# Group 2's attention keys through the seven-product scheme of the queries and keys stage, with each softmax placed behind the next combination's splits

## The chip, the cores and the metric

One core of a Trainium2 chip runs the whole kernel. The metric is the device time of one execution in microseconds (us); lower is better. TensorE (PE in the profile) multiplies; VectorE (DVE) and ScalarE (ACT) do elementwise work; GpSimd (POOL) does little here and issues some DMAs; SyncE (SP) issues nearly all other DMAs, in order.

## The reference

One decoder block on 1024 tokens of width 1024, in float32: a normed and modulated input `h` is projected by one wide matrix; a retention branch (4 heads) and a dilated sliding-window attention branch run beside each other and are merged by sigmoid gates; a squared-ReLU MLP follows. What matters here is the attention branch and its projections:

```python
ATT_GROUPS = ((128, 1), (512, 4), (2048, 16))     # (window, dilation) of three groups of 4 heads, head width 128
proj = h @ w_in                                    # queries, keys, values of every head, and the gates
for gi, (win, dil) in enumerate(ATT_GROUPS):
    aq, ak, av = parts[4 + 3 * gi], parts[5 + 3 * gi], parts[6 + 3 * gi]
    o, lse = dilated_group(heads(aq, 4), heads(ak, 4), heads(av, 4), tab, win, dil)
wts = softmax(stack(lses), axis=0)                 # the three groups of a head are weighed against each other
att = einsum('gbhs,gbhsd->bshd', wts, o_all)
# inside dilated_group, on the tokens of one residue class modulo the dilation:
s = einsum('bhrnid,bhrnjd->bhrnij', qs, kb) * dh ** -0.5 + bias     # masked to the band
e = exp(s - max(s));  den = sum(e);  lse = max + log(den)
```

## The kernel before, in words

**Precision.** Every large product is computed as three products of split operands: a number is split in a high part (a rounded copy, made on ScalarE) and a low part (the rest, a subtraction on VectorE), and `mm3` (lines 203 to 211) adds weight-low x input-high, weight-high x input-low and weight-high x input-high in PSUM. So each operand that TensorE reads costs one ScalarE and one VectorE operation first: a *split*. A matmul here has 128 x 128 weights and up to 512 columns.

**Stages.** Values first; then `queries_keys` (one long step); then values of the retention; then retention chunk by chunk; then attention; then output projections, merge and MLP.

**The queries and keys stage** computes the retention's queries and keys, all attention queries and a part of the gates in pairs of 256 output columns. A pair is one 2 x 2 block product by a scheme of seven products instead of eight (class `Blocks`, `ORDER`): each product is 4 slices of 3 matmuls, 84 matmuls of 512 columns for a pair; VectorE makes the sums of weight blocks and puts the results together. `PAIRS` is the order of the 18 pairs, written by hand as a string; `a_load` loads the weights of a pair two pairs ahead; `a_out` stores queries of attention to the DRAM tensors `aq_d`, in the order of tokens that their group needs.

**The attention stage** goes twice through the same steps, once for each pair of heads (`pair` 0 and 1; `a` is the head in the pair, `g` the group). A *combination* is (g, a), in the order (1,0), (1,1), (2,0), (2,1), (0,0), (0,1). `att_step` for combination i issues 8 slices of 6 matmuls for its keys (`proj_gen`) and, woven in between from the third slice on (`weave` with `lag=2`), the score matmuls of the combination before (`scores_gen`; bias added by VectorE out of PSUM). Then `k_split` splits the new keys out of PSUM, and `scores_end` does the softmax of the combination before: maximum on VectorE, its negation `ng`, eight exponentials on ScalarE (`P<-P,ng`). Behind the second head of a group, `stats_out` sends the row statistics through DRAM. The first `cover_step` (a projection of gates, n = 0) covers the scores of the last combination; then come the weights of the groups, the scaling of the probabilities, and the products with the values in the further cover steps.

**Order.** Nothing is scheduled by a planner: each engine runs its instructions in the order in which the Python code issues them. Class `Steps` decides when weights and queries are split: `following` runs at the start of a step and issues the splits for the next step, and of the weights that lead the step behind that one. Loads (`raw`, three buffers) are issued when the load three places earlier has been split. SP executes them in order with all other DMAs, so a DMA that waits holds up those behind it.

**Result sums.** 32 DMAs that add up parts of the retention's result (`result_sum`, DRAM to DRAM, issued by POOL) are handed out by `with_sums`: two in each projection of the attention stage.

PSUM in this stage: two double banks for projections (`ps_mm`), four single banks for scores and transposes (`ps_s`). Splits of queries and keys live in a ring of eight buffers (`ring`).

Of the kernel before, what the change touches and what calls it, by code (L numbers as in the profile page):

```python
# [11 lines left out]
F32 = mybir.dt.float32  # L12
# [128 lines left out]
def block_kernel(ctx, tc, io, stop=None, dbg=None):  # L141
# [434 lines left out]
    def with_sums(gen):  # L576

        return at(at(gen, 1, result_sum), 5, result_sum)
# [192 lines left out]
    aq_d = {(p, g, a): dram.tile([P, S], F32, name=f"aqd{p}{g}{a}") for p in range(2) for g in range(3) for a in range(2)}  # L771
    h12_d = [dram.tile([P, 2, 512], F32, name=f"h12d{m}") for m in range(4)]
# [363 lines left out]
    PAIRS = [{"r": r_pairs, "a": a_pairs, "g": g_pairs}[i].pop(0) for i in "rargrargrargrargaa"]  # L1136
# [3 lines left out]
    def a_load(q, part):  # L1140
        pair = PAIRS[q]
        src = io[{"g": "w_gate2", "a": "w_aq"}.get(pair[0]) or f"w_r{pair[1]}"]
# [22 lines left out]
    def a_out(q, n, x, y=None):  # L1165
# [6 lines left out]
        if pair[0] == "a" and pair[1] == 1:  # L1172
            o = OA[q][i].rearrange("p (r n i) -> p r n i", r=4, n=2)[:, :, t, :]
            view = lambda z: z.rearrange("p (i r) -> p r i", r=4)
        elif pair[0] == "a" and pair[1] == 2:
            o = OA[q][i].rearrange("p (r i) -> p r i", r=8)[:, :, 64 * t:64 * t + 64]
            view = lambda z: z.rearrange("p (i r) -> p r i", r=8)
# [7 lines left out]
        if n in ("12", "21"):  # L1185
            if pair[0] == "g":
                dst = gate_d[GATES[2 * pair[1] + i]]
            elif pair[0] == "a":
                dst = aq_d[pair[2], pair[1], i]
            else:  # L1190
# [292 lines left out]

    def k_split(pair, g, a, ps):
# [266 lines left out]
    combos = [(g, a) for g in (1, 2, 0) for a in range(2)]  # L1751

    def att_step(pair, i):

        g, a = combos[i]

        def body(*args):
            ps = ps_mm(f"ak{pair}{i}")
            gen = with_sums(proj_gen(ps, args[-1]))
            if i == len(combos) - 2:  # L1760
                v_fetch(pair, 0)
            if i > 0:
                last = combos[i - 1]
                weave(gen, NK, scores_gen(pair, *last), len(SB[last[0]]), lag=2)
# [11 lines left out]
            else:  # L1776

                gen = at(at(gen, 3, args[0]), NK - 1, lambda: k_split(pair, g, a, ps))
                weave_pv(gen, NK - 1, 0, 2)
            if i == 0:  # L1780
                A["st"] = A["p"].tile([P, 3, 8, 4], F32, tag="st", name=f"st{pair}")
                bias_load(pair)
            if i > 0 or pair == 0:
                k_split(pair, g, a, ps)
            if i > 0:
                scores_end(pair, *last)
                if last[1] == 1:
                    stats_out(pair, last[0])
        return body

    def cover_step(pair, n):
# [4 lines left out]
        def body(*args):  # L1796
            ps = ps_mm(f"gate0{i}")
            gen = with_sums(proj_gen(ps, args[-1]))
            if n == 0:
                v_fetch(pair, 1)  # L1800
                weave(gen, 6, scores_gen(pair, *combos[-1]), len(SB[0]), lag=2, rest=False)
                drain(gen)
                v_split(pair, 0, False)
                scores_end(pair, *combos[-1])
# [38 lines left out]
    for pair in range(2):  # L1843
        for i, (g, a) in enumerate(combos):
            steps.add(att_step(pair, i),
                      [wsplit(io["w_ak"][g * 4 + 2 * pair + a])] +
# [955 lines left out]
```

## Time and profile before

| | us |
|---|---|
| runs shown (3): lowest, median, highest | 2182.08, 2183.38, 2184.13 |
| profiled execution, whole | 2182.64 |
| its span, first to last instruction | 2180.9 |
| TensorE busy in it | 2156.0 |
| VectorE busy | 1491.7 |
| ScalarE busy | 942.8 |

The profiled execution is the one whose rows are quoted; its span is what its rows add up to, and 1.7 us lie around it. Rows of the order in time give start, duration, engine, line of the kernel, operation, output <- inputs, and in brackets the idle time of that engine just before with what ended it. Rows of groups end with busy us, mean ns of one, and the idle time before them.

### The profile page before, as it was taken

How to read it: one execution, taken by the hardware profiler on the slowest of the kernel's cores; microseconds unless marked ns; L12 is line 12 of the kernel's file. 1: busy time of each engine (PE TensorE's matmuls, PEld its weight loads, DVE VectorE, ACT ScalarE, POOL GpSimd, SP SyncE). 2: the span in 40 equal slices, each digit the busy share in tenths (PEclk: the TensorE clock that was granted, in tenths of full speed). 3: DMA queues.
4: the chain of work that ended last, by engine and by line, in shares of the span. 5: the costliest groups of instructions: out<-in, count | busy, mean ns of one | idle time of the engine just before them, and what ended most of it. 6: DMA issues, size and time to landing. Idle time of an engine off the chain costs nothing. (4 is left out here: it accounts for less than half of the span.)

```text
span 2180.9 us, 27323 instructions
## 1 busy us (share of the span) xinstructions
PE 2156.0 (99%) x10084; PEld 1791.6 (82%) x10084; DVE 1491.7 (68%) x2333; ACT 942.8 (43%) x1729; POOL 164.0 (8%) x195
## 2 busy tenths in 40 slices
PE   8999999999999999999999999999999999999998
PEld 6888888888878888888888888888778888888887
DVE  5985777774467877854655644776876665877855
ACT  5553323323434544544644625434454545533413
POOL 0001111100012212211100000001000000000003
PEclk9999999999999999999999999999999999999999
DMA  9859998844685555557763275654254435645322
GB/s 383 289 209 297 296 298 257 243 119 174 237 301 170 198 174 194 181 172 190 184 167 108 81 268 189 224 186 139 65 182 150 153 136 194 249 137 175 111 87 78
DMA packets 160881, 416.78 MB, mean 191 GB/s; under 512 B 27749, under 2 KB 55660, under 8 KB 157676
## 3 DMA queue, kind: packets, MB, share of 16 engines
q1 hardware_dynamic: 151416, 368.67, 47.9%
q0 software_dynamic: 9008, 46.14, 9.9%
q8 instruction: 79, 1.29, 0.2%
q14 instruction: 54, 0.44, 0.1%
q10 hardware_dynamic: 324, 0.23, 0.0%
HBM read 319.93 MB, written 156.13 MB: 218 GB/s over the span
## 5 line engine op out<-in xcount | busy, mean ns | idle before, releaser
L207 PE MATMUL qap<-hh,qaw 128*128 128x512 f32 x216 | 84.0, 389 | 0.0
L209 PE MATMUL qap<-hl,qaw 128*128 128x512 f32 x216 | 84.0, 389 | 0.0
L211 PE MATMUL qap<-hh,qaw 128*128 128x512 f32 x216 | 84.0, 389 | 0.0
L617 POOL TENSOR_TENSOR j<-qk,j 128x512 fp32r<-128x512 f32 x32 | 43.2, 1351 | 412.4 <-ACT j L616 393.8
L2122 POOL TENSOR_TENSOR accnf<-accnf,sqnf 128x256 f32<-128x256 f32 (+1 forms) x18 | 16.6, 922 | 609.9 <-ACT sqnf L2118 609.9
L2226 ACT ACTIVATE a<-a 128x512 f32<-128x512 f32 x48 | 30.3, 631 | 73.7 <-DVE a L2225 73.7
L1542 ACT ACTIVATE P<-P,ng 128x128 f32<-128x128 f32 (+1 forms) x96 | 42.0, 439 | 36.6 <-DVE ng L1539 36.6
L2434 ACT CAST w2h<-w2s 128x512 fp32r<-128x512 f32 x36 | 22.4, 622 | 78.7 <-DVE w2s L2472 78.7
L264 DVE TENSOR_TENSOR fw<-w1r,fw 128x512 fp32r<-128x512 f32 x48 | 32.9, 688 | 33.6 <-ACT fw L254 33.6
L1957 DVE TENSOR_TENSOR rwl<-rwl,rwh 128x1024 fp32r<-128x1024 f32 x25 | 30.2, 1220 | 29.1 <-ACT rwh L1987 29.1
L207 PE MATMUL fp<-h2h,fw 128*128 128x512 f32 x128 | 50.0, 391 | 0.0
L211 PE MATMUL fp<-h2h,fw 128*128 128x512 f32 x128 | 49.8, 389 | 0.0
L209 PE MATMUL fp<-h2l,fw 128*128 128x512 f32 x128 | 49.8, 389 | 0.0
L207 PE MATMUL roa<-rh,rwl 128*128 128x512 f32 x128 | 49.8, 389 | 0.0
L209 PE MATMUL roa<-rl,rwh 128*128 128x512 f32 x128 | 49.8, 389 | 0.0
L211 PE MATMUL roa<-rh,rwh 128*128 128x512 f32 x128 | 49.8, 389 | 0.0
L652 ACT COPY sm<-sT 128x128 f32<-128x128 f32 x32 | 8.5, 266 | 93.7 <-PE sT L640 93.7
L207 PEld LDWEIGHTS qap<-hh,qaw 128*128 128x128 f32 x216 | 40.5, 188 | 8.5
L209 PEld LDWEIGHTS qap<-hl,qaw 128*128 128x128 f32 x216 | 40.5, 188 | 8.4
L211 PEld LDWEIGHTS qap<-hh,qaw 128*128 128x128 f32 x216 | 40.5, 188 | 8.4
L2122 POOL TENSOR_TENSOR accn<-accn,sqn 128x512 f32<-128x512 f32 x12 | 15.5, 1293 | 386.1 <-ACT sqn L2118 386.1
L1947 ACT ACTIVATE rh<-rl 128x512 fp32r<-128x512 f32 x56 | 31.7, 623 | 23.4 <-PE roc L209 8.4
(3097 smaller groups left out, 7251.4 us busy)
## 6 DMA issues: line engine op xcount, KB each, us to landing
v<-vd SPq DMA_DIRECT2D x32, 512.0 KB, 4.5
raw<-in_w_ada_dram SPq DMA_DIRECT2D x32, 512.0 KB, 5.3
w1r<-in_w_ff_dram SPq DMA_DIRECT2D x32, 512.0 KB, 4.6
yt<-y POOLq DMA_DIRECT2D x24, 512.0 KB, 7.6
xsd<-as SPq DMA_DIRECT2D x24, 512.0 KB, 2.8
w2r<-in_w_ff2s_dram SPq DMA_DIRECT2D x24, 512.0 KB, 6.9
em<-in_w_ada_dram SPq DMA_DIRECT2D x16, 512.0 KB, 10.2
wrvs<-in_w_rv_dram POOLq DMA_DIRECT2D x16, 512.0 KB, 10.0
```

The lines of the kernel that those rows point to most:

```text
L207: nc.tensor.matmul(o, wl, xh, start=first, stop=False, skip_group_check=skip)
L209: nc.tensor.matmul(o, wh, xl, start=False, stop=False, skip_group_check=skip)
L211: nc.tensor.matmul(o, wh, xh, start=False, stop=last, skip_group_check=skip)
L264: nc.vector.tensor_sub(t[:, 512:], src, fv(t[:, :512]))
L617: nc.gpsimd.tensor_sub(t[:, 1], src, fv(t[:, 0]))
L652: nc.scalar.copy(sm, ps[:, :C])
L1542: nc.scalar.activation(v, v, AF.Exp, bias=ng[:, blk:blk + 1], accum_out=st[:, g, blk, 2 + a:3 + a])
L1947: nc.scalar.activation(hi, fv(lo), AF.Copy, scale=sign)
L1957: nc.vector.tensor_sub(lo, fv(lo), fv(hi))
L2122: (nc.vector if f == 7 else nc.gpsimd).tensor_add(G["acc", key], G["acc", key], sq)
L2226: nc.scalar.activation(o, o, AF.Relu)
L2434: nc.scalar.copy(hi, src)
```

## The change

Group 2's keys are no longer projected in the attention stage. `PAIRS` gets two more pairs, "k", one for each pair of heads; their weights come from a new input `w_ak2`, their results go to the new DRAM tensors `ak_d`, and the attention stage loads and splits them from there (`k_prep`), as it does with queries. That takes the host for the scores of two combinations away, so the projections of group 0's keys are cut in halves of four slices (`att_first`, `att_second`), and each half carries the scores of one combination, from its second slice on (`lag=1`). The softmax of a combination (`scores_end`) isn't issued at the end of the step that made its scores but at the start of the next one, behind the splits that `following` issues there (`scores_done`). `with_sums` hands out three result sums in a projection instead of two.

```diff
@@ -575,7 +575,7 @@
 
     def with_sums(gen):
 
-        return at(at(gen, 1, result_sum), 5, result_sum)
+        return at(at(at(gen, 1, result_sum), 3, result_sum), 5, result_sum)
 
     hd = {}
     NG = H * NC
@@ -769,6 +769,7 @@
 
     va_d = [dram.tile([S, 512], F32, name=f"vad{g}") for g in range(3)]
     aq_d = {(p, g, a): dram.tile([P, S], F32, name=f"aqd{p}{g}{a}") for p in range(2) for g in range(3) for a in range(2)}
+    ak_d = {(p, a): dram.tile([P, S], F32, name=f"akd{p}{a}") for p in range(2) for a in range(2)}
     h12_d = [dram.tile([P, 2, 512], F32, name=f"h12d{m}") for m in range(4)]
     xn, wa = [], []
 
@@ -1133,13 +1134,14 @@
     r_pairs = [("r", t, h) for h in range(H) for t in "qk"]
     a_pairs = [("a", g, p) for p in range(2) for g in range(3)]
     g_pairs = [("g", i) for i in range(len(GATES) // 2)]
-    PAIRS = [{"r": r_pairs, "a": a_pairs, "g": g_pairs}[i].pop(0) for i in "rargrargrargrargaa"]
+    k_pairs = [("k", 2, p) for p in range(2)]
+    PAIRS = [{"r": r_pairs, "a": a_pairs, "g": g_pairs, "k": k_pairs}[i].pop(0) for i in "rargrarkrargrarkgaga"]
     NA = len(PAIRS)
     OA = {}
 
     def a_load(q, part):
         pair = PAIRS[q]
-        src = io[{"g": "w_gate2", "a": "w_aq"}.get(pair[0]) or f"w_r{pair[1]}"]
+        src = io[{"g": "w_gate2", "a": "w_aq", "k": "w_ak2"}.get(pair[0]) or f"w_r{pair[1]}"]
         i = 2 * pair[1] + pair[2] if pair[0] == "a" else pair[-1]
         if q == 0 or q % 2 == 0 and part == 2:
             r = x4(f"wa{q}{part}")
@@ -1169,10 +1171,10 @@
             OA[q] = [x4(f"qa{q}{i}") for i in range(2)]
         i, t = int(n[0]) - 1, int(n[1]) - 1
         o, view = OA[q][i][:, 512 * t:512 * t + 512], lambda z: z
-        if pair[0] == "a" and pair[1] == 1:
+        if pair[0] in "ak" and pair[1] == 1:
             o = OA[q][i].rearrange("p (r n i) -> p r n i", r=4, n=2)[:, :, t, :]
             view = lambda z: z.rearrange("p (i r) -> p r i", r=4)
-        elif pair[0] == "a" and pair[1] == 2:
+        elif pair[0] in "ak" and pair[1] == 2:
             o = OA[q][i].rearrange("p (r i) -> p r i", r=8)[:, :, 64 * t:64 * t + 64]
             view = lambda z: z.rearrange("p (i r) -> p r i", r=8)
         f = AF.Sigmoid if pair[0] == "g" else AF.Copy
@@ -1187,6 +1189,8 @@
                 dst = gate_d[GATES[2 * pair[1] + i]]
             elif pair[0] == "a":
                 dst = aq_d[pair[2], pair[1], i]
+            elif pair[0] == "k":
+                dst = ak_d[pair[2], i]
             else:
                 return
             nc.sync.dma_start(dst, OA[q][i])
@@ -1479,6 +1483,15 @@
             nc.scalar.mul(hi, raw, QSCALE)
             nc.vector.scalar_tensor_tensor(lo, raw, QSCALE, fv(hi), op0=ALU.mult, op1=ALU.subtract)
             A["q", g, a] = (hi, lo)
+        return prep
+
+    def k_prep(pair, a):
+
+        def prep(raw):
+            hi, lo = ring(f"kh{pair}2{a}"), ring(f"kl{pair}2{a}")
+            nc.scalar.copy(hi, raw)
+            nc.vector.tensor_sub(lo, raw, fv(hi))
+            A["k", 2, a] = (hi, lo)
         return prep
 
     def k_split(pair, g, a, ps):
@@ -1748,20 +1761,23 @@
                 done += 1
         drain(main)
 
-    combos = [(g, a) for g in (1, 2, 0) for a in range(2)]
-
-    def att_step(pair, i):
-
-        g, a = combos[i]
+    scored = []
+
+    def scores_done():
+
+        while scored:
+            pair, g, a = scored.pop()
+            scores_end(pair, g, a)
+            if g > 0 and a == 1:
+                stats_out(pair, g)
+
+    def att_step(pair, a):
 
         def body(*args):
-            ps = ps_mm(f"ak{pair}{i}")
+            ps = ps_mm(f"ak{pair}1{a}")
             gen = with_sums(proj_gen(ps, args[-1]))
-            if i == len(combos) - 2:
-                v_fetch(pair, 0)
-            if i > 0:
-                last = combos[i - 1]
-                weave(gen, NK, scores_gen(pair, *last), len(SB[last[0]]), lag=2)
+            if a == 1:
+                weave(gen, NK, scores_gen(pair, 1, 0), len(SB[1]), lag=2)
             elif pair == 0:
                 args[0](1, True)
                 for _ in range(4):
@@ -1775,17 +1791,40 @@
                 args[0](3)
             else:
 
-                gen = at(at(gen, 3, args[0]), NK - 1, lambda: k_split(pair, g, a, ps))
+                gen = at(at(gen, 3, args[0]), NK - 1, lambda: k_split(pair, 1, 0, ps))
                 weave_pv(gen, NK - 1, 0, 2)
-            if i == 0:
+            if a == 0:
                 A["st"] = A["p"].tile([P, 3, 8, 4], F32, tag="st", name=f"st{pair}")
                 bias_load(pair)
-            if i > 0 or pair == 0:
-                k_split(pair, g, a, ps)
-            if i > 0:
-                scores_end(pair, *last)
-                if last[1] == 1:
-                    stats_out(pair, last[0])
+            if a == 1 or pair == 0:
+                k_split(pair, 1, a, ps)
+            if a == 1:
+                scored.append((pair, 1, 0))
+        return body
+
+    HALF = NK // 2
+
+    def att_first(pair, a):
+
+        def body(*args):
+            A["kp"] = ps_mm(f"ak{pair}0{a}")
+            A["kg"] = with_sums(proj_gen(A["kp"], args[-1]))
+            done = (1, 1) if a == 0 else (2, 1)
+            if a == 1:
+                v_fetch(pair, 0)
+            scores_done()
+            weave(itertools.islice(A["kg"], HALF), HALF, scores_gen(pair, *done), len(SB[done[0]]), lag=1)
+            scored.append((pair, *done))
+        return body
+
+    def att_second(pair, a):
+
+        def body(*args):
+            done = (2, 0) if a == 0 else (0, 0)
+            scores_done()
+            weave(A["kg"], HALF, scores_gen(pair, *done), len(SB[done[0]]), lag=1)
+            k_split(pair, 0, a, A["kp"])
+            scored.append((pair, *done))
         return body
 
     def cover_step(pair, n):
@@ -1798,10 +1837,11 @@
             gen = with_sums(proj_gen(ps, args[-1]))
             if n == 0:
                 v_fetch(pair, 1)
-                weave(gen, 6, scores_gen(pair, *combos[-1]), len(SB[0]), lag=2, rest=False)
+                scores_done()
+                weave(gen, 6, scores_gen(pair, 0, 1), len(SB[0]), lag=2, rest=False)
                 drain(gen)
                 v_split(pair, 0, False)
-                scores_end(pair, *combos[-1])
+                scores_end(pair, 0, 1)
                 weights(pair)
                 for a in range(2):
                     pscale(0, a)
@@ -1841,13 +1881,23 @@
             nc.sync.dma_start(gate_d[i], t)
 
     for pair in range(2):
-        for i, (g, a) in enumerate(combos):
-            steps.add(att_step(pair, i),
-                      [wsplit(io["w_ak"][g * 4 + 2 * pair + a])] +
-                      ([(aq_d[pair, *combos[i - 1]], q_prep(pair, *combos[i - 1]))] if i > 0 else []),
-                      manual=("late" if pair else True) if i == 0 else False)
+        def q_load(g, a):
+            return aq_d[pair, g, a], q_prep(pair, g, a)
+
+        def k_load(a):
+            return ak_d[pair, a], k_prep(pair, a)
+
+        def w_load(g, a):
+            return wsplit(io["w_ak"][g * 4 + 2 * pair + a])
+
+        steps.add(att_step(pair, 0), [w_load(1, 0)], manual="late" if pair else True)
+        steps.add(att_step(pair, 1), [w_load(1, 1), q_load(1, 0)])
+        steps.add(att_first(pair, 0), [w_load(0, 0), q_load(1, 1)])
+        steps.add(att_second(pair, 0), [q_load(2, 0), k_load(0)])
+        steps.add(att_first(pair, 1), [w_load(0, 1), q_load(2, 1), k_load(1)])
+        steps.add(att_second(pair, 1), [q_load(0, 0)])
         for n in range(len(COVER[pair])):
-            more = [(aq_d[pair, *combos[-1]], q_prep(pair, *combos[-1]))] if n == 0 else []
+            more = [q_load(0, 1)] if n == 0 else []
             steps.add(cover_step(pair, n), more + [wsplit(io["w_gate"][len(COVER[0]) * pair + n])], manual={2: True, 3: "late"}.get(n, False))
 
 
@@ -2768,7 +2818,8 @@
         "w_rv": _vblocks(w[:, 2048:4096]),
         "w_rg": _cols(w[:, 4096:6144]),
         "w_aq": _pairs(att[:, :, 0].reshape(1024, 1536)),
-        "w_ak": _cols(att[:, :, 1].reshape(1024, 1536)),
+        "w_ak": _cols(att[:, :2, 1].reshape(1024, 1024)),
+        "w_ak2": _pairs(att[:, 2, 1]),
         "w_av": _vcols(att[:, 0, 2], 512),
         "w_av2": _vblocks(att[:, 1:, 2].reshape(1024, 1024)),
         "w_gate": _cols(gates(i for c in COVER for i in c)),
```

## The prediction

> **What bounds the kernel now.** I read the first page, then the busy time by stretches of 100 us, then the list of what TensorE waited for, then the order in time on four queues around the attention scores.
>
> ```profile
> span 2180.9 us, 27323 instructions
> PE 2156.0 (99%) x10084; PEld 1791.6 (82%) x10084; DVE 1491.7 (68%) x2333; ACT 942.8 (43%) x1729; POOL 164.0 (8%) x195
> L207 PE MATMUL qap<-hh,qaw 128*128 128x512 f32 x216 | 84.0, 389 | 0.0
> 400.00:500.00 100.00, 100.00 (x443) 82.81 (x442) 74.32 (x117) 29.38 (x52) 6.80 (x10) 1.00 0.54 154
> 1000.00:1100.00 100.00, 99.66 (x562) 85.68 (x561) 59.87 (x109) 58.67 (x133) 11.19 (x17) 1.00 0.74 189
> 1100.00:1200.00 100.00, 99.87 (x527) 85.38 (x526) 54.56 (x79) 46.49 (x125) 3.52 (x5) 1.00 0.44 130
> PE kv L207 <- ACT state L739: 1.0, 1, 1.0
> PE sc L209 <- DVE kl L1489: 0.4, 1, 0.4
> ```
>
> In the rows by stretches the columns are the stretch, its length, then busy us and count for PE, PEld, DVE, ACT, POOL, then granted clock, DMA share, GB/s. TensorE is busy 99% of the span, and all of 400 to 500 (queries and keys); from 1000 to 1200 (scores, softmax) it is idle 0.5 us, and its longest wait for a score operand in the whole span is 0.4 us. So a matmul removed there is time removed, as long as what feeds TensorE keeps up. The 389 ns of a matmul is its latency: 443 matmuls of 512 columns fill 100 us, so one costs 100/443 = 0.226 us. Taking 389 ns would promise 9.3 us where 5.4 are to be had.
>
> **The change part by part.** *Products.* Four key projections of group 2 (two heads, two pairs), 8 x 6 = 48 matmuls each, leave the attention stage: 192. Two pairs of 7 x 12 = 84 enter the queries and keys stage: 168. Net 24 fewer: 24 x 0.226 = **-5.4 us**; split, -43.4 in attention and +37.9 in the earlier stage.
>
> *Does the earlier stage pay only that?* A pair takes 84 x 0.226 = 19.0 us of TensorE.
>
> ```profile
> L264 DVE TENSOR_TENSOR qaw<-wa,qaw 128x512 fp32r<-128x512 f32 x32 | 21.2, 684 | 2.2 <-ACT qaw L254 2.2
> L1182 DVE TENSOR_TENSOR qa<-qat,qap 128x512 f32<-128x512 f32 x21 | 15.6, 744 | 0.4
> ```
>
> A key pair gives VectorE 7 low parts, 4 weight sums and 5 result steps, 16 operations of at most 0.74 us: 11.8 of its 19.0 us, 62%, under the 74% at which this stage leaves TensorE no gap. Its loads and the stores to the new DRAM tensors are hidden by the two pairs of lead (38 us) that each load has. Cost nothing; if that cover fails it is a few tenths of VectorE lag per pair.
>
> *Removed in attention beside matmuls:* four weight splits and four key splits out of PSUM; *added:* four splits of keys read back from DRAM, of the same size; four loads of weights become four loads of keys. The load on ScalarE and VectorE falls a little in sum, but its time falls more. That is the term that matters.
>
> *The chain of splits and softmaxes.* Call the first half of the projection of group 0, head 0, H1 (with the scores of group 1, head 1, written (1,1)), its second half H2 (scores (2,0)), head 1's halves H3 (scores (2,1)) and H4 (scores (0,0)), the first gate step C0 (scores (0,1)). The order in time on TensorE, DVE, ACT and SP, before, gives the lengths:
>
> ```profile
> 969.84 0.62 PE L207 MATMUL ak<-hh,raw_8107l 128*128 128x512 f32 x2
> 973.94 0.28 PE L207 MATMUL sc<-kh,ql 128*128 128x256 f32 x1
> 983.60 0.62 PE L207 MATMUL ak<-hh,raw_8244l 128*128 128x512 f32 x2
> 997.30 0.62 PE L207 MATMUL ak<-hh,raw_8268l 128*128 128x512 f32 x2
> 1024.79 0.62 PE L207 MATMUL gate<-hh,raw_8498l 128*128 128x512 f32 x2
> 971.31 1.21 DVE L1489 TENSOR_TENSOR kl<-ak,kh 128x1024 fp32r<-128x1024 f32 x1
> 972.44 0.68 DVE L1534 TENSOR_REDUCE st<-P 128x4 f32<-128x512 f32 x1
> 999.74 1.21 DVE L1537 TENSOR_REDUCE st<-P 128x8 f32<-128x1024 f32 x1
> 1026.09 1.23 DVE L1489 TENSOR_TENSOR kl<-ak,kh 128x1024 fp32r<-128x1024 f32 x1 [1.23 <-ACT kh L1488]
> 970.04 1.01 ACT L1488 CAST kh<-ak 128x1024 fp32r<-128x1024 f32 x1 [2.56 <-PE ak L211]
> 974.48 0.40 ACT L1542 ACTIVATE P<-P,ng 128x128 f32<-128x128 f32 x1 [2.13 <-DVE ng L1539]
> 978.01 1.04 ACT L1479 ACTIVATE qh<-raw 128x1024 fp32r<-128x1024 f32 x1
> 978.96 1.04 ACT L197 CAST raw_8268h<-raw 128x1024 fp32r<-128x1024 f32 x1
> 1001.19 0.40 ACT L1542 ACTIVATE P<-P,ng 128x128 f32<-128x128 f32 x1 [2.63 <-DVE ng L1539]
> 1004.29 1.05 ACT L1479 ACTIVATE qh<-raw 128x1024 fp32r<-128x1024 f32 x1
> 991.73 0.62 SPq L1605 DMA_DIRECT2D std<-st  x1
> 995.97 0.38 SPq L1606 DMA_DIRECT2D stn<-std  x1
> ```
>
> A full step is 13.76 us (969.84 to 983.60), 13.70 the next, and 27.49 for the two from 997.30 to 1024.79; less 24 x 0.226 for half a projection, H1 to H4 last 8.33, 8.27, 8.27 and 8.36: C0 starts 33.2 us after H1. C0's scores begin behind three of eight slices, 4.10 us in (969.84 to 973.94), and need the key split of (0,1): at 37.3. Before, that split was done at 1027.3, 1.6 us ahead of its need (1024.79 + 4.10 = 1028.9).
>
> Now the other queues, from the instruction order of the changed kernel. From a maximum to its first exponential: 2.04 us in group 1 (972.44 to 974.48), 1.45 in group 2 (999.74 to 1001.19). Eight exponentials: 3.53 (974.48 to 978.01) and 3.10 (1001.19 to 1004.29). A split costs 0.95 per high part in a row, 1.13 per low part (971.31 to 972.44). Times from H1's start:
> - DVE in H1: low part of keys (1,1) from 1.47 (971.31 - 969.84), then lows of queries and keys (2,0) and of the next weights, 4 x 1.13 = 5.99; maximum of (1,0); its exponentials run 8.0 to 11.6.
> - H2: behind them on ACT the highs of queries and keys (2,1), the last low starts 2.0 later and takes 1.13, then maximum (2.04): exponentials of (1,1) start 5.17 after the former end, and run 16.7 to 20.3.
> - H3: keys (0,0), then queries (0,0) on ACT; VectorE does both lows by 3.31 later, then 1.45: exponentials of (2,0), 25.0 to 28.1.
> - H4: queries (0,1) and *two* gate weights, lows done 4.12 later, 1.45: exponentials of (2,1), 33.7 to 36.8. Behind them stands the split of keys (0,1): high to 37.8, low to 39.1.
>
> The first score of C0 uses the high at once and the low 0.1 us later: TensorE waits from 37.4 to 39.1, **+1.65 us**, if every load is in time. The chain never pauses: each softmax waits for the splits put ahead of it, and those for the exponentials ahead of them, 8.3 to 8.7 us a turn against TensorE's 8.3. Queued behind the waiting matmul is all of C0. Elsewhere I find cover: H1's scores come after two slices (2.73 us), and the split of keys (1,1) ends 1.47 + 1.23 = 2.70 in; PSUM has four score buffers, so late bias additions hold nobody.
>
> *Loads.* Three raw buffers serve the splits, and SP issues in order.
>
> ```profile
> DMA to landing us min/median/max: 3.4/6.2/9.9
> ```
>
> (Raw loads between 940 and 1200.) The softmax statistics store of group 1 stands on SP ahead of the load of the second of those gate weights: it waits for the exponentials' end (20.3), the read-back follows 4.24 later (991.73 to 995.97), the load goes at about 25.0 and lands at 31.2 at the median. ACT wants it at 28.1 + 1.9 = 30.0: **+1.2**. Ends: 0 for 3.4 us to landing, +4.9 for 9.9. The weights split in H1 is similarly between 0 and +2.9; I take +0.3. For the second pair of heads:
>
> ```profile
> 1122.60 0.62 PE L207 MATMUL ak<-hh,raw_9379l 128*128 128x512 f32 x2
> 1123.84 1.23 DVE L1489 TENSOR_TENSOR kl<-ak,kh 128x1024 fp32r<-128x1024 f32 x1 [1.80 <-ACT kh L1488]
> DMA to landing us min/median/max: 4.5/4.5/4.5
> ```
>
> Its keys (1,1) are split 0.23 us earlier in the step (1.24), so +1.4; the load in the gate weights' place (issued at 1149.58) landed in 4.5 us, so nothing is added. Stalls: 1.65 + 1.2 + 0.3 + 1.4 = **+4.5 us**, from 3.1 (all loads in time) to 13 (all at 9.9).
>
> *Third result sum in each projection.* These go on POOL's queue.
>
> ```profile
> L572 POOL DMA_DIRECT2D yt<-y x9 | 7.5, 830 | 58.1 <-DMA yt<-y 37.5 <-DMA yt<-yt 20.5
> ```
>
> POOL waited 58.1 us for earlier sums to land, so offering them sooner changes little; nothing reads them before the later stage. Cost nothing; without that cover, load times as above.
>
> *After C0* comes the softmax of (0,1), the weights of the groups and the scaling, and two steps later TensorE transposes the scaled probabilities.
>
> ```profile
> 1027.42 2.01 DVE L1530 TENSOR_REDUCE st<-P 128x7 f32<-128x1792 f32 x1
> 1040.43 0.17 DVE L1539 TENSOR_SCALAR ng<-st 128x8 f32<-128x8 f32 x1
> 1046.02 2.58 DVE L1645 TENSOR_SCALAR P<-P,wt 128x128 f32<-128x128 f32 x10
> 1038.64 0.62 PE L207 MATMUL gate<-hh,raw_8599l 128*128 128x512 f32 x2
> ```
>
> From the low split of (0,1): about 7 us until TensorE has written the last of four score banks, 0.7 for its bias, 2.2 for the maximum, 8.2 (1040.43 to 1048.60) to the end of scaling, 18 in all. TensorE has the rest of C0 (13.85 - 4.10, from 1024.79 and 1038.64) and 48 matmuls more (10.8), 20.6. I add nothing.
>
> The sum: -5.4 + 4.5 = -0.9 us on the profiled execution's 2182.64, which is 2181.7. The median of the runs shown, 2183.38, is 0.74 above it: **2182.5**. (0.2%, about what a measurement of this kernel can tell from no change, is 4.4 us.)
>
> **A rule of the skill against the change.** The clock first:
>
> ```profile
> 0.00:10.00 10.00, 4.17 (x6) 0.47 (x6) 1.69 (x5) 3.76 (x6) 0.20 (x4) 1.00 0.80 266
> 2170.00:2181.00 11.00, 2.83 (x20) 2.30 (x19) 4.71 (x11) 1.64 (x4) 1.44 (x2) 0.73 0.49 165
> ```
>
> Idle for 5.8 of 10 us the granted clock stayed 1.00; in the last stretch, idle 8.2 of 11, it fell to 0.73. So a stall of about 6 us or more may cost clock behind it. The Trainium skill ("TensorE: Matmul & The Clock Gate", Part 1) says that one idle window of about 3.4 us halves the clock until about 3.4 us of work have passed; by it a long stall would cost an estimated 1.7 us more. My expected stall (3.1 us) is below either.
>
> **The rivals.** *The chain keeps up.* TensorE never waits: the whole -5.4 shows, 2183.4 - 5.4 = 2178.0. For it: today's margin of 1.6 us, and VectorE and ACT only 60% busy. Against: busy share says nothing of a chain that alternates between the two. Chance 0.21.
>
> *Loads late in the shortened stage (the other side).* The same loads fall in 33 us where they had 55, beside the sums; at 9.9 us to landing the first pair stalls 1.65 + 2.9 + 4.9 = 9.4 us, the second, at 7 us to landing, about 1.4 + 2 = 3.4: 12.8 - 5.4 = +7.4, 2190.8. It decides from 9.8 us of stall in all. For it: a DMA share of 0.74 in 1000 to 1100 already. Against: 6.2 at the median. Chance 0.20.
>
> *The clock falls behind a stall.* By the rows, one stall near 6 us in the first pair (3 more than forecast), then half speed for as long as in the last stretch, some 2 us: -0.9 + 3 + 2 = +4.1, 2186.6, still within 0.2%. Chance 0.07.
>
> *The change doesn't do what it says.* The earlier stage isn't held by TensorE any more, and each new pair costs 3 us or more above its matmuls: 2182.5 + 6 = 2188.5. Against: 100.00 of 100 busy beside heavier pairs. Chance 0.04.
>
> **How the numbers follow.** Forecast 0.48 and clock 0.07 make "same" 0.55; faster 0.21; slower 0.20 + 0.04 = 0.24. The forecast's own range is 2181 (all loads in time) to 2187 (loads near 9 us). Reaching to the first rival at 2178.0, and into the second as far as 2189, leaves out 0.17 or so.
>
> **What would show it.** Right: 24 matmuls fewer; the new key pairs 19.0 us each without a gap; H1 to H4 near 8.3 us; in the list of TensorE's waits one for the low key split in C0 of each pair, 3.1 and 1.4 us, with an exponential row or a gate weight ahead of it on ACT. Wrong: no such wait (first rival), a wait of 6 us and more with ACT idle for a raw load (second), or gaps in the queries and keys stage (the last).

## The result and the profile after

The changed kernel takes 2192.53 us (median of 6 runs, 2190.76 to 2194.61) against 2182.82 us for the kernel before in the same runs: a ratio of 1.0044, 95% interval [1.0031, 1.0057]. It is slower by 9.7 us, where 0.9 us less was forecast (2182.5 against the 2183.38 of the runs shown), and lies above the range of 2178 to 2189. Its profiled execution is 2192.05 us with a span of 2190.3 us, 9.4 longer than before.

The first page of the changed kernel:

```profile
span 2190.3 us, 27355 instructions
PE 2156.0 (98%) x10060; PEld 1791.3 (82%) x10060; DVE 1510.5 (69%) x2361; ACT 948.9 (43%) x1743; POOL 163.8 (7%) x195
```

There are 24 matmuls fewer, as there should be, and yet TensorE is busy for the same 2156.0 us: some matmuls took longer. The stretches say which (stretch, length, busy us and count of PE, PEld, DVE, ACT, POOL, granted clock, DMA share, GB/s):

```profile
400.00:500.00 100.00, 100.00 (x442) 82.79 (x442) 74.20 (x116) 28.21 (x50) 7.22 (x11) 1.00 0.61 174
1000.00:1100.00 100.00, 92.36 (x503) 79.49 (x504) 59.12 (x102) 55.52 (x143) 11.54 (x17) 0.95 0.80 217
1100.00:1200.00 100.00, 98.04 (x558) 84.80 (x557) 63.98 (x85) 57.02 (x134) 8.01 (x12) 0.98 0.68 189
```

From 1000 to 1200 TensorE is idle for 7.64 + 1.96 = 9.60 us, against 0.47 before, and the granted clock is 0.95 and 0.98 in place of 1.00. What TensorE waited for, from the list of waits of the whole span (total us, times, longest):

```profile
PE sc L207 <- ACT kh L1501: 6.6, 2, 5.6
PE sc L209 <- DVE kl L1502: 2.9, 4, 1.0
PE kv L207 <- DVE kl L666: 1.3, 2, 0.7
PE rg L207 <- DVE vr L1322: 0.8, 1, 0.8
```

The first two are the key splits of the scores. The wait before the first C0 score has the high part (`kh`) as releaser and lasts 5.6 us; before, the longest wait for a score operand was 0.4.

**The earlier stage.** All matmuls of the queries and keys products, as one group with the first and last start, of the changed kernel:

```profile
L211 PE MATMUL qap<-hh,qaw x240: 389/389/389, 181.3 to 558.7; 128*128 128x512 f32 x120
```

and of the kernel before:

```profile
L211 PE MATMUL qap<-hh,qaw x216: 389/389/389, 180.6 to 519.9; 128*128 128x512 f32 x108
```

377.4 us against 339.3: 38.1 more, where +37.9 was forecast. This stage pays its matmuls and nothing else.

**The first gate step of the first pair.** In the order in time, TensorE, DVE, ACT and SP of the changed kernel (start us, us, engine, line, operation, in brackets the idle time before and its releaser):

```profile
1012.67 0.28 PE L207 MATMUL sc<-kh,ql 128*128 128x256 f32 x1
1013.97 0.38 PE L209 MATMUL sc<-kl,qh 128*128 128x256 f32 x1 [1.02 <-DVE kl L1502]
1047.89 0.61 PE L211 MATMUL gate<-hh,raw_8719h 128*128 128x512 f32 x2
1054.13 0.58 PE L207 MATMUL sc<-kh,ql 128*128 128x256 f32 x1 [5.63 <-ACT kh L1501]
1055.39 0.58 PE L209 MATMUL sc<-kl,qh 128*128 128x256 f32 x1 [0.68 <-DVE kl L1502]
1010.90 1.89 DVE L1532 TENSOR_TENSOR P<-sc,bias 128x512 f32<-128x512 f32 x3 [8.37 <-DMA bias<-biasd]
1012.70 1.22 DVE L1502 TENSOR_TENSOR kl<-ak,kh 128x1024 fp32r<-128x1024 f32 x1
1041.46 1.03 ACT L197 CAST raw_8719h<-raw 128x1024 fp32r<-128x1024 f32 x1
1046.31 1.05 ACT L197 CAST raw_8799h<-raw 128x1024 fp32r<-128x1024 f32 x1 [3.82 <-DMA raw<-in_w_gate_dram]
1050.00 0.40 ACT L1555 ACTIVATE P<-P,ng 128x128 f32<-128x128 f32 x1 [2.63 <-DVE ng L1552]
1053.09 0.99 ACT L1501 CAST kh<-ak 128x1024 fp32r<-128x1024 f32 x1
1032.78 0.63 SPq L1618 DMA_DIRECT2D std<-st  x1
1039.03 0.37 SPq L1619 DMA_DIRECT2D stn<-std  x1
1039.50 0.53 SPq L85 DMA_DIRECT2D raw<-in_w_gate_dram  x1
```

Read from the bottom: SP reads the statistics back at 1039.03, 6.25 us after storing them, and only then issues the second gate weight's load; it lands at 1046.31, when ACT has waited 3.82 us for it; its split, the exponentials of (2,1) from 1050.00 and the key split at 1053.09 follow one behind the other; TensorE waits 5.63 + 0.68 us. At the top, a loss that was forecast to be covered: VectorE waits 8.37 us for the bias, and behind its bias additions stands the low key split of (1,1), for which TensorE waits 1.02 us in H1.

**Behind the wait.** The same kernel in stretches of 3.41 us:

```profile
1047.47:1050.88 3.41, 1.03 (x5) 0.53 (x3) 3.38 (x5) 0.88 (x5) 0.00 (x0) 1.00 1.05 405
1050.88:1054.29 3.41, 0.16 (x1) 0.16 (x1) 1.58 (x5) 3.41 (x14) 0.81 (x1) 0.50 1.02 308
1054.29:1057.71 3.42, 2.74 (x9) 2.25 (x10) 3.42 (x4) 0.73 (x1) 0.00 (x0) 0.50 0.78 137
1057.71:1061.12 3.41, 3.41 (x12) 2.93 (x12) 2.06 (x4) 2.29 (x10) 0.51 (x1) 0.50 0.49 112
1187.41:1190.83 3.42, 1.60 (x9) 0.96 (x8) 1.87 (x2) 2.47 (x6) 0.00 (x0) 1.00 0.07 6
1190.83:1194.24 3.41, 3.41 (x13) 2.83 (x12) 3.38 (x5) 0.56 (x3) 0.00 (x0) 0.50 0.61 144
1194.24:1197.65 3.41, 3.41 (x21) 3.00 (x21) 1.39 (x3) 3.41 (x15) 0.00 (x0) 1.00 0.94 322
```

TensorE's clock is halved for three such periods in the first pair, in which it works 0.16 + 2.74 + 3.41 = 6.31 us, and for one in the second, behind only 1.82 us of idle time (0.95 for the high part, 0.88 for the low). At half speed these 9.72 us of work do what takes 4.86 us at full speed.

**The sum.** 24 matmuls -5.4; idle time between 1000 and 1200 +9.1 (9.60 - 0.47); half clock +4.9; the two waits at the start of retention (`kv`, `rg`) some +0.7 (from 640 to 700 TensorE was idle 2.0 us before and is 2.7 now). That is +9.3, and the span grew by 9.4.

### The profile page after: what moved, and what is told of

The parts are those of the page before. It is cut to its first block, busy times and chain, and to the rows that moved or that the text cites. A ratio compares the mean times of both kernels' runs of the same rounds, so it can differ in the third digit from the quotient of the medians.

```text
span 2190.3 us, 27355 instructions
## 1 busy us (share of the span) xinstructions
PE 2156.0 (98%) x10060; PEld 1791.3 (82%) x10060; DVE 1510.5 (69%) x2361; ACT 948.9 (43%) x1743; POOL 163.8 (7%) x195
## 5 line engine op out<-in xcount | busy, mean ns | idle before, releaser
L207 PE MATMUL qap<-hh,qaw 128*128 128x512 f32 x240 | 93.4, 389 | 0.0
L209 PE MATMUL qap<-hl,qaw 128*128 128x512 f32 x240 | 93.4, 389 | 0.0
L211 PE MATMUL qap<-hh,qaw 128*128 128x512 f32 x240 | 93.4, 389 | 0.0
L207 PEld LDWEIGHTS qap<-hh,qaw 128*128 128x128 f32 x240 | 45.0, 188 | 9.4
L209 PEld LDWEIGHTS qap<-hl,qaw 128*128 128x128 f32 x240 | 45.0, 188 | 9.3
L211 PEld LDWEIGHTS qap<-hh,qaw 128*128 128x128 f32 x240 | 45.0, 188 | 9.3
L292 DVE TENSOR_TENSOR qat<-qat,qap 128x512 f32<-128x512 f32 x20 | 13.7, 687 | 46.7 <-PE qap L211 42.8
L264 DVE TENSOR_TENSOR qaw<-wa,qaw 128x512 fp32r<-128x512 f32 x60 | 40.0, 686 | 7.5 <-ACT qaw L254 7.5
```

What stands on the lines that cost most here:

```text
L207: nc.tensor.matmul(o, wl, xh, start=first, stop=False, skip_group_check=skip)
L209: nc.tensor.matmul(o, wh, xl, start=False, stop=False, skip_group_check=skip)
L211: nc.tensor.matmul(o, wh, xh, start=False, stop=last, skip_group_check=skip)
L264: nc.vector.tensor_sub(t[:, 512:], src, fv(t[:, :512]))
L292: nc.vector.tensor_sub(u, u, b)
```

## The experiments

All edits are to the changed kernel, except in the last experiment. Ratios are to the kernel before, which ran at 2182.5 to 2182.9 us in each set.

### The second gate weight one step later

```diff
 def att_second(pair, a):      # body
+            if a == 1:
+                args[0](1)
-        steps.add(att_second(pair, 1), [q_load(0, 0)])
+        steps.add(att_second(pair, 1), [q_load(0, 0)], manual="late")
```

> The second of the two gate weights that the last half step split ahead of the softmax of (2,1) is split one step later. Theory (a chain of splits and softmaxes, made longer in the first pair of heads by the late load of that weight, and half clock behind each wait): the softmax starts some 4.7 us earlier in the first pair, 1.15 in the second; the waits in the first gate step fall from 6.9 to about 2.2 us and from 2.3 to about 1.1; with 0 to 4 us of half clock saved, 2192.5 becomes 2183 to 2187. Rival (only the late load hurts, the chain by itself has room): the first pair's wait goes altogether and the second's stays at 2.3. Rival (the loss lies in the earlier stages or in load traffic in general): no change, 2192.

Measured: 2182.60 us, ratio 1.0002 [0.9993, 1.0011]. Taking one late load, and the split behind it, out of the chain was worth 9.9 us by the medians (9.6 against the kernel before of each set). What is left on TensorE:

```profile
1048.76 0.38 PE L207 MATMUL sc<-kh,ql 128*128 128x256 f32 x1 [1.09 <-ACT kh L1501]
1050.02 0.56 PE L209 MATMUL sc<-kl,qh 128*128 128x256 f32 x1 [0.88 <-DVE kl L1502]
1182.70 0.39 PE L209 MATMUL sc<-kl,qh 128*128 128x256 f32 x1 [0.87 <-DVE kl L1502]
```

The 1.97 us in the first pair halve the clock behind them (1050.1 to 1053.5), the 0.87 in the second do not.

### Key split (0,1) ahead of the exponentials of (2,1)

```diff
 def att_second(pair, a):
-            scores_done()
+            if a == 0:
+                scores_done()
             weave(...)
             k_split(pair, 0, a, A["kp"])
+            if a == 1:
+                scores_done()
```

> In the last half step the split of keys (0,1) is issued ahead of the softmax of (2,1), not behind it. Theory: the split no longer waits for the exponentials: in the second pair it is done before its need, no wait and no half clock (3.9 us saved); in the first pair ACT still waits for the late gate weight, so the wait falls from 6.9 to about 3.8 us. 2192.5 becomes 2184 to 2186; the softmaxes come 2 us later, so up to 1 us may come back where the scaled probabilities are transposed. Rival (only the late load hurts): the second pair's wait doesn't change, time 2189 to 2192.

Measured: 2188.53 us, 1.0032 [1.0019, 1.0045], above what was expected. The key wait falls to 2.4 us in the first pair and goes in the second, but the softmax of (2,1) now runs later, with it the softmax of (0,1) and the copy of the gate projection out of PSUM, for which TensorE waits 1.3 us in the first pair and 2.7 in the second. The chain handed the wait on.

### The scores of (0,1) behind six slices of the gate step

```diff
-                weave(gen, 6, scores_gen(pair, 0, 1), len(SB[0]), lag=2, rest=False)
+                weave(gen, 8, scores_gen(pair, 0, 1), len(SB[0]), lag=5, rest=False)
```

`lag` counts slices from zero: with `lag=2` the scores begin behind the third slice, with `lag=5` behind the sixth. Some of the expectations count as `lag` does.

> In the first gate step the scores of (0,1) begin behind six of the eight slices, not three: 4.1 us more cover, with the chain left as it is. Theory: the first pair's wait falls from 6.9 to 2.8 us, the second's goes with its half clock; 2192.5 becomes 2182 to 2185. A rival by which the chain sets the pace of all that follows (softmax of (0,1), scaling): the wait only moves to the first transposes of scaled probabilities, and the time stays above 2189.

Measured: 2187.49 us, 1.0022 [1.0011, 1.0032]: again more than expected. Three slices more (4.1 us) leave 2.2 + 0.9 us of key waits in the first pair, and 1.0 us in each pair appears for the same copy of the gate projection. The profiled execution, the slowest of the eight (2189.93), also waits 2.8 us for `kv` at the start of retention, where the edit changes nothing, and the clock is halved once there (682.9 to 686.3).

### Filling the idle time with matmuls

```diff
                 scores_done()
+                gen = at(gen, 2, lambda: [proj_mm(ps, args[-1], [2]) for _ in range((5, 1)[pair])])
                 weave(gen, 6, ...)
```

> The first gate projection of each pair of heads takes its third slice several times more (5 times, 30 matmuls, in the first pair, once, 6 matmuls, in the second), right ahead of the first scores of (0,1), so TensorE works through most of its wait; that gate's values are then not the reference's. The chain isn't touched: the scores begin when they began. If the half clock behind each wait comes from the idle time: granted clock 1.00 throughout, 2.6 + 1.6 us saved, 2188. If it comes from anything else: 2192.5.

Measured: 2189.43 us, 1.0031 [1.0019, 1.0042]; the values of that gate are then not the reference's. TensorE does 36 matmuls, 8.1 us, more, and by the medians the kernel is 3.1 us faster than the changed one. Its stretches:

```profile
1000.00:1100.00 100.00, 100.00 (x559) 86.34 (x558) 59.81 (x104) 57.69 (x148) 11.59 (x17) 1.00 0.80 217
1100.00:1200.00 100.00, 98.66 (x559) 85.11 (x559) 67.32 (x89) 57.69 (x141) 8.04 (x12) 1.00 0.65 185
```

Clock 1.00 in both: the half clock came from the idle time, since work in its place removes it.

### Two result sums again

```diff
-        return at(at(at(gen, 1, result_sum), 3, result_sum), 5, result_sum)
+        return at(at(gen, 1, result_sum), 5, result_sum)
```

> Undoes one part of the change: each projection again offers two result sums to POOL's queue in place of three. By my theory the sums have no part in the loss: the second gate weight lands late because its load is issued late (it stands on SP behind the statistics' read-back), so it still lands near 1046 us and the time stays at 2191 to 2193.5 us. By the rival (the sums' transfers crowd the loads of the shortened stage) the load takes 4 to 5 us to landing in place of 6.8, the wait of TensorE in the first gate step of pair 0 falls from 6.9 to about 4.5 us, and the time falls to 2188 to 2190 us.

Measured: 2191.58 us, 1.0039 [1.0025, 1.0053], with single runs from 2188.4 to 2195.9. In the profiled execution (2189.56) the statistics are back 4.8 us after their store and ACT waits only 1.65 us for the gate weight, TensorE 3.49 + 0.88 for the keys, which is the rival's picture. But the edit is not what did it. In both traces POOL issues the same thirteen sum DMAs between 980 and 1060, each within 1.2 us of its time in the other trace, because POOL is held until earlier ones have landed. So the same transfers run beside the load, the sums offered sooner have no part in the loss of the first pair, and the shorter way of the statistics is scatter; in the second pair TensorE is idle for the same 1.82 us. The four runs lie 7.4 us apart, and their median, 1 us lower, can't be told from the changed kernel's.

### The statistics' store one softmax later

```diff
 def scores_done():
+        while stats_due:
+            stats_out(*stats_due.pop())
         ...
-                stats_out(pair, g)
+                stats_due.append((pair, g))
```

> The store and read-back of the softmax statistics is put one softmax later on SP, so that it no longer stands ahead of the load of the second gate weight. By my theory the 3.8 us that ScalarE waits for that load in pair 0 go (issue near 1033 us in place of 1039.5), TensorE's wait for the keys of (0,1) there falls from 6.9 us to about 3, the stretch at half clock behind it stays: 2187 to 2189.5 us. If the late load is only where a wait of the chain shows, the split still comes late and the time stays above 2191 us. If the statistics are now late for the groups' weights, a wait appears before the transposes and gives back 2 us or more.

Measured: 2187.54 us, 1.0020 [1.0010, 1.0029], as expected. SP's queue and the two gate weights on ACT:

```profile
1035.94 0.33 SPq L85 DMA_DIRECT2D raw<-in_w_gate_dram  x1
1037.34 0.63 SPq L1618 DMA_DIRECT2D std<-st  x1
1041.33 1.03 ACT L197 CAST raw_8719h<-raw 128x1024 fp32r<-128x1024 f32 x1
1042.27 1.04 ACT L197 CAST raw_8795h<-raw 128x1024 fp32r<-128x1024 f32 x1
```

The load goes 3.6 us earlier and ACT no longer waits for it. TensorE's wait for the keys is 2.14 + 0.87 = 3.0 us: this is the stall of the chain alone, for which the forecast had 1.65 + 0.3. The clock still halves behind it (1051.6 to 1055.0), and behind 1.82 us in the second pair.

### Each softmax ahead of the splits again

```diff
 def att_step(pair, a):
                 scored.append((pair, 1, 0))
+                scores_done()
 def att_first / att_second:
             scored.append((pair, *done))
+            scores_done()
```

> Undoes the other part of the change: each softmax stands again ahead of the next combination's splits, the halved steps and the keys of group 2 stay as changed. Then the exponentials of (2,1) and both gate weights still stand ahead of the split of keys (0,1), but each softmax starts some 4 us earlier and the splits of queries and keys (2,0) come some 2.3 us too late for the scores in the second half step. By my theory (one chain, its length the same in either order) the wait moves from the first gate step to the half steps, 2 to 3 us in each pair and with a stretch of half clock behind it: 2183 to 2188 us. If the order is what cost the time, it falls to 2180 us or less; if the order is what keeps the loss small, the half steps each wait some 6 us and the time is above 2195 us.

Measured: 2200.26 us, 1.0078 [1.0063, 1.0092]. My expectation fell: the new order is not what costs the time, it keeps the loss small. TensorE's waits in the first pair:

```profile
1032.51 0.30 PE L207 MATMUL sc<-kh,ql 128*128 128x128 f32 x1 [2.63 <-DVE ql L1484]
1033.55 0.33 PE L209 MATMUL sc<-kl,qh 128*128 128x128 f32 x1 [0.75 <-DVE kl L1493]
1051.88 1.22 PE L207 MATMUL gate<-hh,raw_8735l 128*128 128x512 f32 x2 [2.83 <-DVE raw_8735l L198]
```

The waits in the half steps are 3.4 us, half of the 6 that went with this outcome, but later in the chain the gate weight's split is late too (2.83, and 1.54 in the second pair), which I hadn't seen, and in all the clock is halved for four periods.

### Moving the scores as well

Four kernels start from the gate weight one step later. The first adds `lag=5` as above and, for the scores of (1,1), `lag=2` in place of 1:

```diff
-            weave(itertools.islice(A["kg"], HALF), ..., lag=1)
+            weave(itertools.islice(A["kg"], HALF), ..., lag=2 - a)
```

> Three edits at once: the second gate weight is split one step later (which alone gave 2182.6 us), the scores of (0,1) begin five slices into the first gate step in place of two, and those of (1,1) two slices in place of one. By my theory no wait of TensorE over 0.5 us is left between 1000 and 1060 us and none over 0.5 us near 1185 us, the granted clock stays at 1.00, and what the 24 matmuls less are worth shows: 2177.5 to 2180 us. By the rival that the chain of splits and softmaxes only passes the wait on, the later scores free the gate projection's PSUM later and TensorE waits there instead: 2181 to 2184 us.

Measured: 2183.26 us, 1.0002 [0.9993, 1.0011]. The key waits are gone, but its list of waits now has

```profile
PE gate L207 <- ACT g00s L1870: 2.8, 1, 2.8
PE gate L207 <- ACT g04s L1870: 1.0, 1, 1.0
```

which is the rival's wait. So the copy was put ahead of the group weights:

```diff
                 scores_end(pair, 0, 1)
+                t = ring(f"g0{i}s", F32)
+                nc.scalar.copy(t, flat(ps))
+                raw_gates.append((i, t))
                 weights(pair)
```

> The three edits of the kernel with the later scores (second gate weight one step later, scores of (0,1) five slices into the first gate step, those of (1,1) two slices in), and its first gate projection is copied out of PSUM by ScalarE between the exponentials of (0,1) and the group weights, in place of behind the weights and the scaling. By my theory the waits of 2.8 and 1.0 us for that copy go, nothing is late in their place, and the 24 matmuls less show for the first time: 2177.5 to 2180.5 us. By the rival that the chain only passes its wait on, the copy makes the scaling late and TensorE waits at the transposes instead: 2181.5 to 2184 us.

Measured: 2183.37 us, 0.9999 [0.9990, 1.0008]: TensorE now waits 1.4 us at the first transpose and 1.7 us at the first product behind it, and in the profiled execution (2185.64, the slowest of eleven) the clock is halved once behind them. With the copy and `lag=3` (`weave(gen, 7, ..., lag=3, ...)`):

> As the kernel before it in this call, but the scores of (0,1) begin three slices into the first gate step (over seven slices), not five: one slice, 1.36 us, later than in the changed kernel. With the second gate weight one step later TensorE waited there 1.09 + 0.88 us; one slice more leaves about 0.6 us, less than the 1.8 us behind which the clock was seen to halve, and the softmax of (0,1) is 2.7 us earlier than with five slices: 2178 to 2181 us. By the rival (the clock halves behind any wait for the key split) the stretch at half clock stays: 2180.5 to 2183 us.

Measured: 2181.46 us, 0.9997 [0.9988, 1.0006]; and without the copy:

> The second gate weight one step later, the scores of (0,1) three slices into the first gate step, those of (1,1) two slices in, and no early copy of the gate projection. With the early copy TensorE waited 1.7 us for ScalarE's copy of the first transposed scores in pair 0, and retention's entry cost about 1.3 us more than before, which left 1.1 us of the 5.4 at the median. If the wait behind the softmax of (0,1) only changes its place, TensorE now waits 1 to 2 us for the gate projection's copy instead, and the time is 2180.5 to 2182.5 us. If the early copy was what made the transposes late, no wait over 1 us is left in either pair: 2178.5 to 2180.5 us.

Measured: 2181.92 us, 0.9995 [0.9986, 1.0004]. The list of waits of the kernel with the copy:

```profile
PE kv L207 <- DVE kl L666: 2.5, 2, 1.9
PE pv L1699 <- ACT pth000(0, 0, 0)_9208 L1679: 1.7, 1, 1.7
PE sc L209 <- DVE kl L1502: 1.2, 2, 0.9
```

and of the one without:

```profile
PE gate L207 <- DVE raw_8719l L198: 2.0, 1, 2.0
PE gate L207 <- ACT g00s L1870: 1.7, 1, 1.7
PE sc L209 <- DVE kl L1502: 1.2, 2, 0.9
```

Both leave the changed kernel 10 to 11 us behind, and neither can be told from the kernel before: of the 5.4 us some 4 are still given back. In the attention stage neither halves the clock, and what is left there are waits at other places of the same chain. In the profiled execution of the kernel with the copy (2183.88, its slowest) the larger part is elsewhere: its `kv` row is the start of retention, where TensorE waits 2.5 us and the clock is halved once (681.6 to 685.0).

### Waits put into the kernel before

```diff
-                weave(gen, NK, scores_gen(pair, *last), len(SB[last[0]]), lag=2)
+                fill = scores_gen(pair, *last)
+                if i % 2:
+                    next(fill)
+                weave(gen, NK, fill, len(SB[last[0]]) - i % 2)
```

> The kernel before, with waits put in on purpose: in each attention step the scores begin behind one slice of the projection in place of three (a wait of about 1.1 us for the key split, four times), or ahead of its first slice (about 1.2 + 1.1 us with one matmul between, six times). Theory: the clock is judged on a fixed grid of 3.41 us, and halves for one period if more than about 1.7 us of the one before was idle; then none of the short waits and some four of the six long ones halve it, each drop is a whole number of 3.41 us away from every other, each lasts 3.4 us, and the time is 2182.9 + 4 x 1.1 + 6 x 2.4 + 4 x 1.7 = about 2208 us. Rival, that only an unbroken idle of some 3.4 us halves it, and that something else halved it in the changed kernel: clock 1.00 throughout, about 2202 us.

Measured: 2212.0 us (one run), 4 above the theory's figure and 10 above the rival's. The clock drops three times, not four; one drop, behind a longer wait than intended, lasts two periods. All three start a whole number of periods apart (959.83, 1127.09, 1161.22: 49 and 10). In stretches laid on the grid that the drops give:

```profile
990.55:993.97 3.42, 2.05 (x9) 1.27 (x7) 0.56 (x1) 1.01 (x1) 0.83 (x1) 1.00 0.99 375
993.97:997.38 3.41, 2.69 (x17) 2.47 (x18) 2.56 (x4) 0.78 (x3) 0.00 (x0) 1.00 0.77 125
1157.81:1161.22 3.41, 1.42 (x11) 1.28 (x11) 2.37 (x3) 1.00 (x1) 0.00 (x0) 1.00 0.01 5
1161.22:1164.63 3.41, 3.41 (x13) 2.83 (x11) 0.75 (x2) 2.60 (x12) 0.00 (x0) 0.50 0.00 0
```

Both places have the same wait, 1.16 us for the high and 0.93 for the low part. At 990 it falls across a border of the grid (1.37 us idle on one side, 0.72 on the other) and the clock stays at 1.00; at 1157 it falls inside (1.99) and the next period runs at 0.50. The rival, unbroken idle time of 3.4 us, is out.

## Why the prediction was wrong

Of stall the forecast had 4.5 us. The trace has 9.1 of idle time in attention (6.3 and 1.8 in the first gate steps, 1.0 in H1), 4.9 of half clock and 0.7 at the start of retention.

- *Products:* right. 24 matmuls fewer, +38.1 us in the earlier stage against +37.9.
- *The chain of splits and softmaxes:* right in its place and its order, one size too small. With the late load out of it the first pair waits 3.0 us against 1.95, the second 1.82 against 1.4.
- *Loads:* the first step that failed. +1.2 was taken for the second gate weight out of a range to +4.9, and TensorE waited 6.3 us in place of 3.1, 3.3 of them for the load. The 0.3 for H1's weights did not show. Against the times reckoned from H1's start (1009.93) the exponentials ahead of the statistics' store ended 2.4 us later, the way to DRAM and back took 2.0 more (6.25 us, not the 4.24 of before), the landing 0.6 more (6.8, not 6.2). The forecast took one value for the way to DRAM and back, from the kernel before; in the eleven traces of kernels with the shortened stage whose statistics are stored right behind their softmax it took 4.3 to 6.9 us. Moving the statistics away brought 5.0 us, moving the weight 9.9 (both with half clock saved).
- *"Late bias additions hold nobody":* wrong. PSUM had room, but the additions are queued on VectorE ahead of the key split (1,1): 1.02 us of TensorE in H1, and the chain behind it starts later.
- *The clock:* the second step that failed, as large as the first. From two stretches of 10 and 11 us I took some 6 us of idle time as what a drop needs, gave it 0.07 and put it at 2 us. It came behind 1.8 us too, and the two drops cost 4.9. Stretches of 10 us average over three periods, and so hide what happens in one.
- *Third result sum:* nothing, and for the reason given: POOL waits for earlier sums to land. *After C0,* "I add nothing" held for the changed kernel, whose list has no such wait; that the stall ahead had made the room is likely, not shown. In the kernels without the stall the waits for the gate projection's copy or the transposes come to 1.7 to 3.9 us.
- *Retention's start* had no term in the sum: +0.7 us.

The row from 0 to 10 us, one of the two behind "some 6 us", was also misread. The clock record of that trace starts at 14.34 us, so the 1.00 is a blank and not a granted clock. The matmuls of the kernel before on either side of 14.3 us (two groups; shortest, median and longest in ns, first and last start) show that it ran at about half speed ahead of it:

```profile
L846 PE MATMUL av<-wv0wh,hh x8: 454/628/796, 11.1 to 14.2; 128*128 128x512 f32 x8
L846 PE MATMUL av<-wv0wh,hl x15: 389/389/398, 14.7 to 23.7; 128*128 128x512 f32 x15
```

In the half-clock stretch of the changed kernel (1057 to 1061) matmuls of this size take the same 628 ns. The clock rival's time has a slip as well: 2186.6 counts the -0.9 twice; 2183.4 + 4.1 is 2187.5.

So the outcome bears the second rival's sign, a wait of more than 6 us with ACT idle for a raw load, with the clock's on top; the chances treated the two as apart, though the first brings on the other. That the second rival's 2190.8 came near is luck: it had 12.8 us of stall and no half clock, the trace has 9.1 and 4.9.

The Trainium skill ("TensorE: Matmul & The Clock Gate", Part 1) says that the clock is judged over a free-running window of 3413 ns. The traces agree to the hundredth of a period: in the changed kernel the first drop (1050.88) and the one in the second pair (1190.83) are 41.00 periods apart. It also says that the clock falls back after an idle window, and here the measurement differs: a window with 1.82 of 3.41 us idle was enough.

## What to carry to other kernels

A chain that alternates between two engines has a length, and this stage, shortened below that length, gave nothing: most edits moved the wait to another place of one chain, and the best came out even. Before a step is shortened, put each DMA round trip on the queue at its worst observed time, from several traces, and look for what stands behind each waiting instruction on its own engine. And price a TensorE wait at more than its length: from about 1.8 us within one period of 3.41 us upward it can halve the clock for the 3.4 us behind it. A granted clock of 1.00 in a stretch where no clock record lies says nothing.

## What the hardware showed

The half clock starts and ends on a fixed grid of 3.41 us. I laid that grid over the traces of all fourteen kernels, from the first clock record to the drop at the end of each, without that drop. Of the full-speed periods with 0.90 us of idle time or more, the 66 with up to 1.66 us were followed by a period at 1.00, and the 19 with 1.82 us or more, broken or not, by one at 0.50. (The drop at the end came behind 0.73 to 2.70 us. TensorE runs matmuls of one column there, for which the modelled busy time says little.) In the attention stage a half-clock stretch lasted one to three periods. One period on the full-speed side, from the kernel with the order of softmax and splits undone, second pair:

```profile
1191.56:1194.97 3.41, 1.87 (x11) 1.47 (x10) 3.41 (x4) 2.23 (x3) 0.00 (x0) 1.00 0.61 138
1194.97:1198.38 3.41, 3.31 (x16) 2.56 (x15) 3.41 (x8) 0.00 (x0) 0.00 (x0) 1.00 0.87 324
```

1.54 us idle, clock unchanged. Counted from the first instruction, the first border of the grid falls between 0.2 and 3.0 us in the fourteen traces. So the same wait can cost its length in one run and 1.7 us more in the next. The start of retention shows it: its code is the same in the twelve traces of the changed kernel and its variants, TensorE was idle there (640 to 720) for 2.3 to 3.7 us, and in two of them the clock was halved once. In line with that, though not shown by these traces alone, the kernel with the copy and `lag=5` ran between 2180.1 and 2185.6 us, the kernel before in the same set between 2181.7 and 2184.0.
